# A shared row of four buffers, copies in dead tiles, and a planner with a corrected forward pass and other durations

## The chip, the cores and the metric

The kernel runs on one core of one Trainium2 chip. The metric is the device time of one execution in microseconds (us), the median of the runs; a profile is taken of one further execution. The engines are TensorE (PE, with its weight loads as PEld), VectorE (DVE), ScalarE (ACT), GpSimd (POOL) and SyncE (SP). DMA transfers are issued from three queues here: SP's, ACT's and POOL's.

## The reference

One pre-norm residual layer with two mixers on the same normalised input, in float32, for 1024 tokens of width 1024:

```python
h = rmsnorm(x, norm_w);  proj = h @ w_in
y_a = (dilated_mixture(q_a, k_a, v_a) * silu(dsa_z)) @ w_up_a      # three windows / dilations, 8 heads of 64
q, k, v = split(silu(causal_conv4(gdn_qkv)));  q, k = l2norm(q) / 8, l2norm(k)
# gated delta rule in chunks of 64, per head (8 heads of 64)
G = cumsum(g);  decay = exp(G_i - G_j) for i >= j
a = (k*beta @ k.T) * decay (strictly lower);  t_inv = inverse(I + a)
u = t_inv @ (v*beta);  w = t_inv @ (k*beta*exp(G));  attn = (q @ k.T) * decay
scan over chunks: v_new = u - w @ S;  o = (q*exp(G)) @ S + attn @ v_new
                  S = S * exp(G_last) + (k*exp(G_last - G)).T @ v_new
y_b = (rmsnorm(o) * silu(gdn_z)) @ w_up_b
out = rmsnorm(x + (sigmoid(gate_a)*y_a + sigmoid(gate_b)*y_b) @ w_out, final_norm_w)
```

## The kernel before

The projections run as units of 128-row weight blocks. A float32 weight is loaded into `wstage`, split into two float16 parts (`whi` on ACT, `wlo` on DVE), and multiplied by the split input in three products (lines 184, 185, 186). A `Feed` object streams these units, and every other stage of the kernel calls `feed.tick(n)` between its own products, so that PE always has unit work between them. Matmuls that stand at lines 184 to 186 are therefore work that fills PE while another stage waits for its operands.

Mixer A (attention) is done first, then mixer B (the delta rule), whose 8 heads are handled in two halves, `hb` 0 and 1. For each half: `decay` builds `gm` from the decays on DVE and sums it on PE (line 1195); `keys_side` and `pairs` build the matrix `a` (in `MT`) and spill it; `solve` inverts the 32 x 32 diagonal blocks on DVE in 31 steps (`stmp`, `X`, working on `As`), scales `X`, makes its negated transpose `T1`, spills both (`u_d`, `t_d`) and reloads them, shaped for PE, as blocks of `MT` (line 1335) and as `T1p` (line 1333). `merge` makes the 64 x 64 inverse from the blocks: `left` multiplies by T1p (line 1350) and DVE writes `Y`; `right` (line 1365) multiplies by Y. `state_parts` multiplies the inverse with the values (`u`, line 1413, PSUM banks G) and with the keys `kbt` (`w`, line 1417, banks S), each in two groups of four tiles. Each group has two u banks, copied out by DVE and spilled on POOL's queue, and two w banks, copied out by ACT and spilled on ACT's queue (lines 1424 to 1429). `values` transposes v and scales it into `rv`, which is spilled. A second call of `pairs` makes q times k in the same PSUM banks (line 1266, `E` on DVE afterwards). Gate units between them write `gst` on ACT and spill it on ACT's queue (`gspb`, lines 948 and 950). In the conv units, `xc` and `ca` (lines 1005 to 1021) are copied by ACT and worked on by DVE.

Buffers come from pools by tag; tiles of one tag share `bufs` buffers in turn, and a tile waits until the one that had the buffer before is read for the last time. The tag `rv` is a row of three buffers of 2 KB a partition; `Y`, `uw` and `rv` share it. `gm` has a tag of its own with two. `As`, `X` and `T1p` have one buffer each; in the second half, the first group's `kbt` lies in As and the second's in X.

PE's instructions stand in the order in which the program is written. The order of DVE, ACT, POOL and SP is made at the end of the file by a planner: `steps_of` gives each instruction a modelled duration (`Step.cost`) and its dependences, buffers included; `fill` places them in time, forward with ranks and then backward for new ranks; `orders_of` does that three times (`PASSES`) and keeps the order whose modelled end is earliest; `set_orders` fixes it. The forward `fill` takes events (time, engine) from a heap. Before, an engine with nothing ready goes either into the heap for the time of its next known instruction, or into the set `blocked`; `known`, which is called when an instruction's last dependence is placed, wakes only engines in `blocked`.

Of the kernel before, what the change touches and what calls it, by code (L numbers as in the profile page):

```python
# [11 lines left out]
F32 = mybir.dt.float32  # L12
# [66 lines left out]
def hybrid_block(ctx: ExitStack, tc: tile.TileContext, A):  # L79
# [1099 lines left out]
    def decay(hb):  # L1179

        for t in range(8):
            if hb == 0 and t < 2:

                if t == 0:
                    room = wst.tile([128, 512], F32, name="x7", tag="x7", bufs=1)
                gm = room[:, 256 * t:256 * t + 256]
            else:
                gm = p2_.tile([128, 256], F32, name="gm", tag="gm", bufs=2)
            gm = gm.bitcast(F16).rearrange("p (l a i) -> p l a i", l=2, i=64)
            TT(gm, bc(gsplit[:, :, t, hb], 64), upto64[:, None, None, :].to_broadcast([128, 2, 4, 64]), ALU.mult)  # L1190
            if t == 0:
                feed.tick(GM_LAG)
            p = bank("G", 2)
            for l in range(2):
                PE.matmul(p[:, :256], lhsT=later16, rhs=gm[:, l].rearrange("p a i -> p (a i)"), start=(l == 0),
                          stop=False)
            PE.matmul(p[:, :256], lhsT=ident_b, rhs=hide_b[:, None, :].to_broadcast([128, 4, 64]),
                      start=False, stop=True)
            SC.activation(E[hb][:, t].rearrange("p a b c -> p (a b c)"), p[:, :256], AF.Exp)
            feed.tick(2)  # L1200
# [138 lines left out]
    def merge(hb, T1p, bsp):  # L1339
# [4 lines left out]
        def left(g):  # L1344
            py = bank("S", 2)
            Y = p2_.tile([128, 16, 32], F32, name="Y", tag="rv", bufs=3)
            for n in range(16):
                for c2 in range(2):
                    r = 64 * c2
# [34 lines left out]
    def state_parts(hb):  # L1384
# [13 lines left out]
        for g in range(2):  # L1398
# [6 lines left out]
            for n in range(8):  # L1405
                t, q, o = n // 2, n % 2, n * 64
                for x in range(2):
                    for r, e in ((0, 0), (1, 1), (0, 1), (1, 0)):
# [6 lines left out]
                        else:  # L1415
                            b = 64 * e
                            PE.matmul(pw[r][b:b + 64, o:o + 64], lhsT=kb[rs, t, 2 * q + e], rhs=Ub, start=(n == 0),
                                      stop=True, skip_group_check=True)
            for x, ps2 in enumerate((pu, pw)):
                for r in range(2):  # L1420
                    c2 = r ^ hb
                    uw = p2_.tile([128, 4, 2, 64], F32, name="uw", tag="rv", bufs=3)
                    with tc.high_priority():
# [9 lines left out]
    def values(hb):  # L1433
        def then(c, vT):
            h0 = 4 * hb + 2 * c

            def turn(t0):
                p = bank("O", 1)
                for tt in range(4):
                    PE.transpose(p[:, tt * 128:tt * 128 + 128],  # L1440
                                 vT[:, 2 * (t0 + tt):2 * (t0 + tt) + 2].rearrange("p c i -> p (c i)"), ident)
                rv = p2_.tile([128, 4, 2, 64], F32, name="rv", tag="rv", bufs=3)
                with tc.high_priority():
# [505 lines left out]
TABLE_NS = 1283  # L1949
TILE_SWITCH_NS = 300  # L1950
QUEUE_NS = 4
# [47 lines left out]
class Step:  # L1999
# [17 lines left out]
    def cost(self):  # L2017
        w, r = [[x for x in self.args if x.write == y] for y in (True, False)]
        n = max(x.cols for x in self.args)
        if self.kind == "InstMatmult":  # L2020
            self.small = tuple(self.ins.tile_size) != (128, 128)
# [22 lines left out]
        elif self.eng == "DVE":  # L2044
            one = len(r) == 1
            self.ns = {"InstMemset": 60 + 0.5 * n, "InstReciprocal": 150 + 6.2 * n, "InstTensorCopy": 160 + 0.55 * n}.get(
                self.kind, 150 + 1.0417 * n)
            if self.kind == "InstTensorScalarPtr":
                self.ns = 150 + 0.53 * n if one else self.ns + 60 * (len(r) > 2)
            self.hold = self.ns - 83  # L2050
        elif self.eng == "ACT":
            self.ns = 130 + 0.9 * n
            if self.kind == "InstActivation":
                self.table = TABLES.get(str(self.ins.func).split(".")[-1], 0)
                self.ns += 25 * (w[0].size == 2) + 30 * (len(r) > 1)
            self.hold = self.ns - 90 + 40 * (len(w) > 1)
            self.ns += 100 * (len(w) > 1)
        else:
            self.hold = self.ns = 100 + 0.85 * n
# [95 lines left out]
def fill(steps, rank, back, given):  # L2155
# [4 lines left out]
    free, moved, due, open_ = [{e: x() for e in order} for x in (float, float, list, list)]  # L2160
    events, blocked, table, small, end = [(0.0, e) for e in order], set(), 0, None, 0.0

    def known(i):
# [3 lines left out]
        elif e not in given:  # L2167
            heapq.heappush(due[e], (ready[i], i))
        if e in blocked:
            blocked.discard(e)  # L2170
            heapq.heappush(events, (max(free[e], ready[i]), e))

# [13 lines left out]
    while events:  # L2186
        t, e = heapq.heappop(events)
        if t < free[e]:
            heapq.heappush(events, (free[e], e))
            continue  # L2190
        if e in given:
# [3 lines left out]
            if left[i]:  # L2195
                blocked.add(e)
                continue
            if ready[i] > t:
                heapq.heappush(events, (ready[i], e))
                continue  # L2200
        else:
# [3 lines left out]
            if not open_[e]:  # L2205
                if due[e]:
                    heapq.heappush(events, (due[e][0][0], e))
                else:
                    blocked.add(e)
                continue  # L2210
# [12 lines left out]
        order[e].append(i)  # L2223
        heapq.heappush(events, (free[e], e))
        passed(s, t, late)
# [132 lines left out]
```

## Time and profile before

| | us |
|---|---|
| runs | 1075.26, 1066.41, 1068.09 |
| median | 1068.09 |
| profiled execution, its own time | 1070.89 |
| its span, first to last instruction | 1069.1 |
| PE's sequence of the second half's merge begins at about | 721.5 |
| PE's products w of the second half end at | 750.4 |

The profile gives for each engine its busy time, for each group of instructions the time one takes and what the engine waited for before it, and for each stretch of time the clock that was granted to PE (1.00 is full). A wait is named by the instruction that waits and by what released it.

### The profile page before, as it was taken

To read this page: it belongs to the slowest core of one execution; us is meant where nothing else is said; L and a number is where in the kernel's file an instruction comes from. 1 tells how busy PE (TensorE), PEld (TensorE's weight loads), DVE (VectorE), ACT (ScalarE), POOL (GpSimd) and SP (SyncE) were. 2 spreads that over 40 slices of the span, in tenths; PEclk is the share of its full clock that TensorE was granted. 3 is DMA by queue.
4 is the path that set the end of the run, shared out by engine and by line. 5 is a ranking of instruction groups with operands and counts; after the bars stand their busy time and mean duration, and the time that the engine had idled before them with its cause. 6 is when DMAs were issued, how large, how long until landed. Compare 5 with 4: busy or idle time off the path is not lost.

```text
span 1069.1 us, 24944 instructions
## 1 busy us (share of the span) xinstructions
PE 1042.0 (97%) x9986; PEld 639.1 (60%) x9986; DVE 877.7 (82%) x2030; ACT 573.0 (54%) x1306; POOL 56.3 (5%) x107
## 2 busy tenths in 40 slices
PE   7999999999999999999999999998899999999997
PEld 5995695765957755866655545544545555444444
DVE  6898987989979889989957986885298768899934
ACT  6446767777766666567635533244244336434523
POOL 0000000000000000000000000110100000000000
PEclk9999999999999999999999999998899999999999
DMA  7144532532624432552336166784685414823132
GB/s 278 62 123 114 140 105 90 134 100 83 188 88 127 123 105 75 145 154 69 95 108 186 59 176 178 262 228 154 209 271 168 147 53 147 324 93 124 58 132 79
DMA packets 99780, 148.53 MB, mean 139 GB/s; under 512 B 31168, under 2 KB 64704, under 8 KB 98512
## 3 DMA queue, kind: packets, MB, share of 16 engines
q1 hardware_dynamic: 69264, 84.64, 27.3%
q0 software_dynamic: 12320, 44.11, 13.1%
q10 hardware_dynamic: 18080, 18.20, 5.0%
q8 instruction: 78, 1.28, 0.5%
q14 instruction: 38, 0.31, 0.1%
HBM read 91.13 MB, written 36.90 MB: 120 GB/s over the span
## 4 chain that ended last, share of the span: by engine, by line
PE 67%; DVE 14%; DMA 7%; issue 5%; ACT 4%; SPq 2%; ACTq 0%; DVEq 0%; POOLq 0%
PE ps_mm L184 16%; PE ps_mm L185 16%; PE ps_mm L186 16%; DMA wstage<-in_w 2%; PE ps_S L185 2%; PE ps_S L184 2%; PE ps_S L186 2%; DVE tl L87 1%; SPq L629 1%; DVE ca L84 1%; PE ps_G L813 1%; ACT sm L803 1%; DVE sm L799 1%; DVE wlo L84 1%; PE ps_G L184 1%
## 5 line engine op out<-in xcount | busy, mean ns | idle before, releaser
L186 PE MATMUL ps_mm<-h_hi,wlo 128*128 128x512 f16 (+1 forms) x552 | 208.8, 378 | 0.0
L184 PE MATMUL ps_mm<-h_hi,whi 128*128 128x512 f16 (+1 forms) x492 | 186.5, 379 | 0.0
L185 PE MATMUL ps_mm<-h_lo,whi 128*128 128x512 f16 (+1 forms) x492 | 186.3, 379 | 0.0
L186 PEld LDWEIGHTS <-wlo 128*128 128x128 f16 x788 | 77.4, 98 | 87.1 <-issue 1.7
L184 PEld LDWEIGHTS <-whi 128*128 128x128 f16 x848 | 83.4, 98 | 69.4 <-issue 1.7
L185 PEld LDWEIGHTS <-whi 128*128 128x128 f16 x848 | 83.3, 98 | 69.6 <-issue 3.4
L803 ACT ACTIVATE sm<-sm,osb 128x128 f32<-128x128 f32 (+1 forms) x160 | 69.3, 434 | 47.0 <-DVE osb L799 46.2
L799 DVE CUSTOM_DVE_ANT_0 sm<-ps_S,amask 128x128 f32<-128x128 f32 (+1 forms) x192 | 59.7, 347 | 6.7 <-PE ps_S L792 6.6
L87 DVE TENSOR_TENSOR tl<-ps_G,th 128x256 f16<-128x256 f32 (+1 forms) x96 | 52.0, 542 | 15.4 <-ACT th L818 14.8
L330 ACT ACTIVATE whi<-wstage 128x512 f16<-128x512 f32 x76 | 46.1, 626 | 31.3 <-DVE wstage L329 9.5
L84 DVE SCALAR_TENSOR_TENSOR wlo<-wstage,whi 128x1024 f16<-128x1024 f32 x42 | 51.0, 1220 | 8.8 <-ACT whi L167 7.3
L167 ACT ACTIVATE whi<-wstage 128x1024 f16<-128x1024 f32 x41 | 42.7, 1054 | 27.7 <-PE ps_mm L185 23.7
L185 PE MATMUL ps_mm<-wlo,h_hi 128*128 128x256 f16 (+1 forms) x256 | 57.3, 246 | 0.0
L84 DVE SCALAR_TENSOR_TENSOR ca<-xc,cw,ca 128x512 f32<-128x512 f32 x72 | 53.8, 747 | 2.5 <-ACT ca L1010 2.2
L84 DVE SCALAR_TENSOR_TENSOR whi<-wstage,whi 128x512 f16<-128x512 f32 x76 | 51.9, 687 | 3.8 <-ACT whi L330 3.4
L329 DVE TENSOR_TENSOR wstage<-wstage 128x512 f32<-128x512 f32 x76 | 52.0, 687 | 0.9
L813 PE MATMUL ps_G<-cons,sm 128*128 128x128 f32 x280 | 47.0, 274 | 2.1 <-ACT sm L803 2.0
L818 ACT CAST th<-ps_G 128x256 f16<-128x256 f32 (+1 forms) x96 | 44.1, 459 | 6.7 <-PE ps_G L813 6.2
L184 PE MATMUL ps_mm<-whi,h_hi 128*128 128x256 f16 (+1 forms) x192 | 46.5, 256 | 0.0
L186 PE MATMUL ps_mm<-whi,h_lo 128*128 128x256 f16 (+1 forms) x192 | 46.2, 255 | 0.0
L184 PE MATMUL ps_mm<-h_hi,wlo 128*128 128x512 f16 x120 | 45.6, 380 | 0.0
L185 PE MATMUL ps_mm<-h_lo,wlo 128*128 128x512 f16 x120 | 45.5, 379 | 0.0
(489 smaller groups left out, 2880.3 us busy)
## 6 DMA issues: line engine op xcount, KB each, us to landing
wstage<-in_w POOLq DMA_DIRECT2D x68, 512.0 KB, 4.5
og<-osb ACTq DMA_DIRECT2D x32, 132.0 KB, 2.4
og<-og SPq DMA_DIRECT2D x32, 132.0 KB, 2.2
gspb<-gst ACTq DMA_DIRECT2D x16, 256.0 KB, 4.3
sga<-gspa SPq DMA_DIRECT2D x8, 512.0 KB, 8.8
wstage<-in_w_up POOLq DMA_DIRECT2D x8, 512.0 KB, 4.7
sgb<-gspb SPq DMA_DIRECT2D x8, 512.0 KB, 4.0
wos<-in_w_out SPq DMA_DIRECT2D x8, 512.0 KB, 4.7
```

What stands on the lines that cost most here:

```text
L84: (eng or V).scalar_tensor_tensor(out, in0, scalar, in1, op0=op0, op1=op1)
L87: (eng or V).tensor_tensor(out, in0, in1, op)
L167: SC.activation(hi[:, 4 * c:4 * c + 4], st, AF.Copy, scale=W_SCALE)
L184: PE.matmul(out, lhsT=wh(k), rhs=mh(k), start=first and i == 0, stop=False, skip_group_check=True)
L185: PE.matmul(out, lhsT=wh(k), rhs=ml(k), start=False, stop=False, skip_group_check=True)
L186: PE.matmul(out, lhsT=wl(k), rhs=mh(k), start=False, stop=last and i == len(ks) - 1, skip_group_check=True)
L329: V.tensor_tensor(self.part[name], self.part[x], self.part[y], ALU.add)
L330: SC.activation(t[:, b, 0], self.part[name], AF.Copy, scale=W_SCALE)
L799: V.tensor_tensor_reduce(P[:, u, :128 * nk], psc[:, u * 256:u * 256 + 128 * nk], mask, -cexp, -NEG, ALU.add, ALU.min, accum_out=osb[:, 256 ...
L803: SC.activation(P[:, u, :128 * nk], P[:, u, :128 * nk], AF.Exp, bias=osb[:, 256 + hd:257 + hd], scale=-1.0, accum_out=osb[:, 260 + hd:261 ...
L813: PE.transpose(pt[:, c:c + 128], P[:, u, i * 128:i * 128 + 128], ident)
L818: SC.copy(th[:, :n], pt[:, :n])
```

## The change

It has four parts.

1. `gm` no longer has two buffers of its own but shares the row `rv`, which now has four buffers in place of three, for gm, Y, uw and rv together.
2. In the second half the w copies of a group go into one tile `ws`, which holds both, in place of two buffers of the row: the first group's in `T1p`, the second's in `As`. The spill then reads from `ws`.
3. The planner's durations: a switch of PE between tile shapes 250 ns (was 300); DVE's copies from PSUM by the slower slope; an additional term (`apart`) for DVE and ACT instructions that read a PSUM tile in single elements with a stride; ACT's instructions with a second output 190 ns more (was 100).
4. The forward pass of `fill`: each engine has a next wake-up time, and an engine that waits for a later time is woken earlier when another of its instructions becomes ready sooner.

The computation is the same.

```diff
@@ decay
-                gm = p2_.tile([128, 256], F32, name="gm", tag="gm", bufs=2)
+                gm = p2_.tile([128, 256], F32, name="gm", tag="rv", bufs=4)
@@ merge, left
-            Y = p2_.tile([128, 16, 32], F32, name="Y", tag="rv", bufs=3)
+            Y = p2_.tile([128, 16, 32], F32, name="Y", tag="rv", bufs=4)
@@ state_parts
+            if hb:
+                ws = p2_.tile([128, 2, 4, 2, 64], F32, name="ws", tag="As" if g else "T1p", bufs=1)
             for x, ps2 in enumerate((pu, pw)):
                 for r in range(2):
                     c2 = r ^ hb
-                    uw = p2_.tile([128, 4, 2, 64], F32, name="uw", tag="rv", bufs=3)
+                    if x and hb:
+                        uw = ws[:, r]
+                    else:
+                        uw = p2_.tile([128, 4, 2, 64], F32, name="uw", tag="rv", bufs=4)
                     with tc.high_priority():
                         (SC.copy if x else V.tensor_copy)(uw, ps2[r].rearrange("p (t q i) -> p t q i", q=2, i=64))
@@ values
-                rv = p2_.tile([128, 4, 2, 64], F32, name="rv", tag="rv", bufs=3)
+                rv = p2_.tile([128, 4, 2, 64], F32, name="rv", tag="rv", bufs=4)
@@ the planner
-TILE_SWITCH_NS = 300
+TILE_SWITCH_NS = 250
@@ Step.cost
+        apart = any(x.psum and x.piece == x.size for x in r) and n >= 256
...
             one = len(r) == 1
-            self.ns = {"InstMemset": 60 + 0.5 * n, "InstReciprocal": 150 + 6.2 * n, "InstTensorCopy": 160 + 0.55 * n}.get(
+            fast = one and not r[0].psum
+            self.ns = {"InstMemset": 60 + 0.5 * n, "InstReciprocal": 150 + 6.2 * n, "InstTensorCopy": 160 + (0.55 if fast else 1.0417) * n}.get(
...
+            self.ns += 0.58 * n * apart
...
-            self.hold = self.ns - 90 + 40 * (len(w) > 1)
-            self.ns += 100 * (len(w) > 1)
+            self.ns += 0.94 * n * apart + 190 * (len(w) > 1)
+            self.hold = self.ns - 90
@@ fill
-    events, blocked, table, small, end = [(0.0, e) for e in order], set(), 0, None, 0.0
+    events, wake, table, small, end = [], {}, 0, None, 0.0
+
+    def at(t, e):
+        if t < wake.get(e, np.inf):
+            wake[e] = t
+            heapq.heappush(events, (t, e))
@@ fill, known
-        if e in blocked:
-            blocked.discard(e)
-            heapq.heappush(events, (max(free[e], ready[i]), e))
+        if e is not None:
+            at(max(free[e], ready[i]), e)
@@ fill, the loop
         t, e = heapq.heappop(events)
+        if t != wake[e]:
+            continue
+        wake[e] = np.inf
         if t < free[e]:
-            heapq.heappush(events, (free[e], e))
+            at(free[e], e)
             continue
...
             if not open_[e]:
                 if due[e]:
-                    heapq.heappush(events, (due[e][0][0], e))
-                else:
-                    blocked.add(e)
+                    at(due[e][0][0], e)
                 continue
```

PE's order is the same in both kernels. The order of the others moves in three places that matter here. Of line numbers, those above 1418 are 5 higher after the change and those of the planner more.

ACT, where the second half's w copies (`uw`, then `ws`) stand with their spills `wn_d` and the gate unit's `gst` and `gspb`. Before:

```order
L1424 COPY uw<-ps_S 128x512
L1426 DMA wn_d<-uw 128x4x128
L1424 COPY uw<-ps_S 128x512
L1426 DMA wn_d<-uw 128x4x128
L1424 COPY uw<-ps_S 128x512
L948 ACTIVATE gst<-ps_mm 128x512
L1426 DMA wn_d<-uw 128x4x128
L950 DMA gspb_11041<-gst 128x512
L1424 COPY uw<-ps_S 128x512
L1426 DMA wn_d<-uw 128x4x128
```

The same place of ACT after the change:

```order
L1429 COPY ws<-ps_S 128x512 x2
L1431 DMA wn_d<-ws 128x4x128 x2
L1429 COPY ws<-ps_S 128x512 x2
L1431 DMA wn_d<-ws 128x4x128 x2
L948 ACTIVATE gst<-ps_mm 128x512
L950 DMA gspb_11039<-gst 128x512
```

The two copies of a group now stand together ahead of their two transfers, and the gate unit's copy and spill stand behind all of them.

DVE at the end of the second half's solve, from the last two steps (`stmp`, `X`) to `T` (T1 in the code); `ca` and `xc` belong to a conv unit, `wlo` to a weight unit. Before:

```order
L87 TENSOR_TENSOR stmp<-As,X 128x31
L84 SCALAR_TENSOR_TENSOR wlo<-wstage,whi 128x1024
L87 TENSOR_TENSOR X<-X,stmp 128x31
L84 SCALAR_TENSOR_TENSOR ca<-xc,cw,ca 128x512
L87 TENSOR_TENSOR X<-X,bsc 128x1024
L84 SCALAR_TENSOR_TENSOR ca<-xc,cw,ca 128x512
L1323 TENSOR_SCALAR T_9508<-X 128x1024
L84 SCALAR_TENSOR_TENSOR ca<-xc,cw,ca 128x512
L84 SCALAR_TENSOR_TENSOR wlo<-wstage,whi 128x1024
```

The same place of DVE after the change:

```order
L87 TENSOR_TENSOR stmp<-As,X 128x31
L1007 COPY xc<-xc 128x3
L87 TENSOR_TENSOR X<-X,stmp 128x31
L87 TENSOR_TENSOR X<-X,bsc 128x1024
L84 SCALAR_TENSOR_TENSOR ca<-xc,cw,ca 128x512
L1323 TENSOR_SCALAR T_9508<-X 128x1024
L84 SCALAR_TENSOR_TENSOR ca<-xc,cw,ca 128x512 x2
L1005 MEMSET xc 128x3
L84 SCALAR_TENSOR_TENSOR wlo<-wstage,whi 128x1024
```

The wlo and the ca that stood between the solve's last steps now stand behind T; with two ca from some steps earlier, four ca, one wlo and a memset that were ahead of T are behind it.

SP's queue at the second half's reloads (`MT` blocks from `u_d`, `T1p` from `t_d`, then the keys `kbt` and gate reloads `sga`). Before:

```order
L1326 DMA u_d_9510<-X 128x1024
L1327 DMA t_d_9511<-T_9508 128x1024
L1335 DMA MT_8544<-u_d_9510 32x32x32 x4
L1333 DMA T1p<-t_d_9511 32x32x32 x2
L1393 DMA kbt<-kb_d_8558 128x1024 x2
```

The same place of SP's queue after the change:

```order
L1326 DMA u_d_9510<-X 128x1024
L1327 DMA t_d_9511<-T_9508 128x1024
L1335 DMA MT_8544<-u_d_9510 32x32x32
L1333 DMA T1p<-t_d_9511 32x32x32 x2
L1335 DMA MT_8544<-u_d_9510 32x32x32 x2
L1393 DMA kbt<-kb_d_8558 128x1024
L1335 DMA MT_8544<-u_d_9510 32x32x32
L1393 DMA kbt<-kb_d_8558 128x1024
```

Both T1p loads now stand behind one MT load in place of four, and the last MT load stands between the two kbt loads.

More of the change, by code (lines that the diff above doesn't have):

```diff
@@ L2195, in fill @@
             if left[i]:
-                blocked.add(e)
                 continue
             if ready[i] > t:
-                heapq.heappush(events, (ready[i], e))
+                at(ready[i], e)
                 continue
@@ L2206, in fill @@
                 if due[e]:
-                    heapq.heappush(events, (due[e][0][0], e))
-                else:
-                    blocked.add(e)
+                    at(due[e][0][0], e)
                 continue
@@ L2223, in fill @@
         order[e].append(i)
-        heapq.heappush(events, (free[e], e))
+        at(free[e], e)
         passed(s, t, late)
```

## The prediction

> **What bounds the kernel now.** I read the page's head first, then the waits of TensorE (PE), then a table of stretches around the two longest waits, then the chain and the queues inside them.
>
> ```profile
> span 1069.1 us, 24944 instructions
> PE 1042.0 (97%) x9986; PEld 639.1 (60%) x9986; DVE 877.7 (82%) x2030; ACT 573.0 (54%) x1306; POOL 56.3 (5%) x107
> PEclk9999999999999999999999999998899999999999
> ...
> PE ps_mm L502 <- DVE nwd L87: 5.2, 1, 5.2
> PE ps_S L1350 <- DMA T1p<-t_d: 3.6, 2, 2.9
> PE ps_S L1266 <- ACT uw L1424: 3.5, 1, 3.5
> PE ps_G L813 <- ACT sm L803: 2.0, 2, 1.4
> PE ps_mm L184 <- ACT gst L948: 1.5, 1, 1.5
> PE ps_O L840 <- DVE tl L87: 1.3, 2, 0.9
> ```
>
> PE is the bound: 1042.0 of 1069.1 us, so at most 27 us can be had by waiting less. The clock row has two digits below 9, side by side, in slices 28 and 29 of 40, 722 to 775 us. The wait rows give total, times and longest: after the 5.2 us of the start, the two largest are a load of T1p that PE's merge waits for, and a copy of ScalarE (ACT) that frees a PSUM bank. The stretches around them (columns: length, busy time of PE, its weight loads, DVE, ACT and POOL with counts, granted clock, DMA share, GB/s):
>
> ```profile
> 650.00:706.00 56.00, 56.00 (x754) 29.09 (x755) 48.55 (x103) 18.45 (x31) 7.78 (x13) 1.00 0.65 213
> 706.00:721.50 15.50, 15.50 (x195) 8.30 (x186) 12.69 (x22) 4.81 (x10) 1.65 (x3) 1.00 1.06 293
> 721.50:724.80 3.30, 0.55 (x3) 0.05 (x1) 1.99 (x4) 2.65 (x6) 0.00 (x0) 1.00 0.99 217
> 724.80:731.60 6.80, 5.95 (x73) 3.26 (x74) 4.91 (x8) 1.48 (x4) 0.00 (x0) 0.50 0.68 266
> 731.60:753.00 21.40, 21.40 (x520) 12.87 (x519) 8.29 (x13) 7.96 (x15) 4.26 (x7) 1.00 0.35 107
> 753.00:755.50 2.50, 0.32 (x3) 0.19 (x2) 0.00 (x0) 0.00 (x0) 0.80 (x2) 1.00 0.91 219
> 755.50:762.30 6.80, 5.45 (x71) 3.14 (x72) 1.29 (x2) 0.59 (x1) 0.56 (x1) 0.50 0.42 144
> ...
> 374.20:534.50 160.30, 157.23 (x1538) 104.09 (x1536) 150.38 (x480) 106.86 (x281) 7.42 (x14) 1.00 0.38 107
> ```
>
> Each wait is followed by 6.8 us at clock 0.50. So a wait costs its own length and a dip. Two ways to size it. By windows: 721.5 to 731.6 is 10.1 us, in which PE did 0.55 us of work at full clock and 5.95/2 at half, so 6.6 us were lost; 753.0 to 762.3 is 9.3 us with 0.32 + 5.45/2 of work, so 6.3 lost; 12.9 in all. By waits: 3.6 + 3.5, and half of 6.8 twice, 13.9. I take 13.5, an estimate between them.
>
> The waits of 1.5 us and less have no dip after them, the shortest one with a dip has 2.9. The Trainium skill, page "TensorE: Matmul & The Clock Gate", Part 1, section on the clock gate, says that the array falls to half rate after at least one whole idle window of about 3.4 us and comes back after a busy one of that length. Here two idle windows would have to lie in waits of 2.9 and 3.5 us, and the trace decides otherwise for the first.
>
> **First part of the change: row of four, copies elsewhere.** No instruction is added or taken away, and the order of PE is the same; what can change is when PE's operands are there. For the second stall, the chain and ACT's rows:
>
> ```profile
> 750.26 0.12 PE ps_S L1417 x8
> ...
> 756.21 0.59 ACT uw L1424
> 756.85 1.98 PE ps_S L1266 x62
> ...
> 744.41 0.59 ACT L1424 COPY uw<-ps_S 128x512 f32<-128x512 f32 x1 [1.44 <-PE ps_S L1417]
> 747.50 0.59 ACT L1424 COPY uw<-ps_S 128x512 f32<-128x512 f32 x1 [2.50 <-DMA wn_d<-uw]
> 751.10 0.59 ACT L1424 COPY uw<-ps_S 128x512 f32<-128x512 f32 x1 [3.02 <-DMA wn_d<-uw]
> 756.21 0.59 ACT L1424 COPY uw<-ps_S 128x512 f32<-128x512 f32 x1 [3.80 <-DMA gspb<-gst]
> ```
>
> The products end at 750.38. Three of the four copies waited for a DMA: the row of three had no free buffer until an earlier spill had read it. That the last row names the gate spill gspb only says which DMA ended last; the two copies before it, held by wn_d, show the kind. With ws the copies of a group have a tile each. As and T1p are dead there: the kbt in As is read by the first group's products, T1p by the merge. In the new order two copies stand in a row, then two DMAs. So both banks are free at 750.38 + 2 x 0.59 = 751.6, and PE wants them at 753.0: 1.4 us to spare. The gst that stood between them comes 0.6 us later at most; its bank is not wanted sooner than ACT's next gst, so I cost it at nothing. The cover is those 1.4 us; if it goes, the stall is the shortfall. What is late next is E (DVE waits for the same L1266 products), which only comes earlier.
>
> ACT had the same wait one half earlier, and DVE paid for it:
>
> ```profile
> 684.11 0.59 ACT L1424 COPY uw<-ps_S 128x512 f32<-128x512 f32 x1 [9.56 <-DMA wn_d<-uw]
> ...
> 685.22 0.17 DVE L1007 COPY xc<-xc 128x3 f32<-128x3 f32 x1 [3.45 <-ACT xc L1008]
> ```
>
> The copies of xc queue behind that copy on ACT, and DVE sat 3.45 us in the middle of the triangular solve. A fourth buffer lets it go by up to 3.45 us; the low end is 0, if the fourth is just as late (gm, Y, rv and u now share the row). I take 3.45, since for this group only four w and four u copies compete in it.
>
> **Second part: the planner moves DVE and SP.** The solve's end and T1p's way:
>
> ```profile
> 702.89 1.22 DVE L84 SCALAR_TENSOR_TENSOR wlo<-wstage,whi 128x1024 f16<-128x1024 f32 x1
> 704.14 0.74 DVE L84 SCALAR_TENSOR_TENSOR ca<-xc,cw,ca 128x512 f32<-128x512 f32 x1
> 705.93 0.75 DVE L84 SCALAR_TENSOR_TENSOR ca<-xc,cw,ca 128x512 f32<-128x512 f32 x1
> 706.60 1.05 DVE L1323 TENSOR_SCALAR T<-X 128x1024 f32<-128x1024 f32 x1
> ...
> 706.08 5.49 DMA u_d<-X
> ...
> 719.54 6.37 DMA T1p<-t_d
> 725.96 1.91 PE ps_S L1350 x62
> ...
> 711.59 5.15 SPq L1335 DMA_DIRECT2D MT<-u_d  x4
> 716.79 3.88 SPq L1333 DMA_DIRECT2D T1p<-t_d  x2
> ...
> t_d<-T SPq DMA_DIRECT2D x1, 512.0 KB, 5.1
> ```
>
> By the order, five instructions and a small memset that stood ahead of T (T1 in the code) now stand behind it: one wlo of 1.22 and four ca of about 0.75 (the wlo and two of the ca are in the rows), 4.2 us. So T, which ended at 707.65, ends at 703.4, and with the 3.45 from above at 700.0. (Two further wlo of 1.22 move into DVE's idle time ahead of the solve; they are left as margin.) Then T1p's way: the spill of T, 5.1 to landing; the T1p issues on SP, 3.88 at most; their landing, 6.37. SP has one MT load ahead of them in place of four, which took 5.15, and that one waits for u_d, spilled before T, so it adds nothing. From T's end that is 15.4 us: T1p is there at 715.4, or at 718.8 without the 3.45. PE wants it at about 722 (0.55 us of work after 721.5): 6.6 or 3.2 us to spare. What covers the load is PE's other work, full in the row 706.00:721.50. The MT loads now behind T1p, and a kbt load that goes between them, wait for two T1p issues and a kbt issue more, at most 3.88 and 1.3 (taken as a quarter of the 5.15), against 4.2 to 7.7 gained; I cost it at nothing. The next to be late would be those MT loads, for the right products. POOL's row of transfers keeps its order but for one or two places, and no term rests on it.
>
> **Third part: everything else that the new costs move.** The decays' gm now take rv buffers.
>
> ```profile
> 588.27 0.69 DVE L87 TENSOR_TENSOR gm<-wide,cons 128x512 f16<-128x512 f16 x1 [0.93 <-PE ps_G L1195]
> ...
> 599.17 0.68 DVE L87 TENSOR_TENSOR rv<-ps_O,bg 128x512 f32<-128x512 f32 x1
> ```
>
> The last gm comes 11 us before the first rv, and what holds it is PE's own product with the gm before, so with four buffers for two it can only come sooner: by the 0.93 of DVE's idle time at most, and PE does not wait for it. The other end is one lap of a buffer held by a spill, ACT's 9.56 above. I take nothing, as no rv, Y or u is alive then. In the attention stretch 374 to 534, and in the one before it, 39 of the 96 tl stand later in the new order and 18 earlier, mostly by one instruction. The waits for sm, gst and tl are 4.8 us in all (2.0 + 1.5 + 1.3, rows above). Bounds: 4.8 gained if all went, as much lost if each doubled. I take 0, the middle.
>
> **Sum.** 13.5 gone, 0 elsewhere. Against its own time, 1070.89 for the profiled execution (span 1069.1 and 1.8 around it), that is 1057.4. The median of the runs is 1068.09, 2.8 below the profiled one. If that difference is a dip less (half of 6.8 is 3.4), the saving is already partly in it and 1057.4 stands; if it is spread over everything, 1068.09 - 13.5 = 1054.6. I take the middle, 1056.0.
>
> **The rivals.** (a) Only one stall goes. For the first: DMA share is 1.06 in 706 to 721.5, so T1p may land late for want of engines, whatever its place in the queue; it decides once the landing takes 3.2 to 6.6 us longer. For the second: 1.4 us to spare is little. Against: the u_d and MT traffic comes earlier too, into 690 to 706, and the row 650.00:706.00 has a share of 0.65. It gives 1056.0 plus 6.3 to 6.6: 1062.5.
>
> (b) The stalls go, the dips stay, because the small 32x32 products and not the waiting bring the clock down. Against: the other half's merge and products lie in 650 to 706, and that row has clock 1.00. It gives 1056.0 + 2 x 3.4 = 1062.8. By the rule of the Trainium skill's page named above, a wait shorter than a whole window would not lower the clock, so the first dip would have such another cause and one dip would stay; that case is in this rival, at 1059.4.
>
> (c) The change doesn't do what it says: the waits move but stay, because the row of four fills as the row of three did and the costs are no nearer the chip's. Time as before, 1068. Against: the ws tiles wait for nothing in the order.
>
> (d) Slower: DVE becomes the bound in the attention stretch. It is busy 150.38 of 160.30, PE 157.23. DVE has 9.9 us of idle time there to make good what is late; if each of the 39 later tl in the two stretches held PE by 0.65, the mean of the two tl waits of before, 25 us would be added and it would be 1056.0 + 25 = 1081. It decides from 23 us of new waits on (1078.8 - 1056.0). Against: PE waited for tl twice in 96 before.
>
> **How the numbers follow.** Chances: my forecast 0.62, (a) 0.17, (b) 0.08, (c) 0.06, (d) 0.07. Faster or slower by over 1% (10.7 us, about what a measurement of this kernel can tell from no change) means up to 1057.4 or from 1078.8. The forecast's own spread is 1051 (all 4.8 of small waits go too) to 1060 (some are added); about 0.54 of its 0.62 lie below 1057.4, and a little of (b). Faster 0.55, within 1% 0.38, slower 0.07. The range has the forecast and rivals (a) and (b) within 1051 to 1064 and leaves out (c), (d) and a few hundredths.
>
> **What would show it.** Right: no PE wait on T1p or on the w copies above 1 us, clock 1.00 from 650 to 780, the T1p load landing before 720, the four w copies in pairs with no idle time for a DMA before the second of each, and DVE's 3.45 at 685 gone. Wrong: a new wait of over 2.4 us anywhere, with its dip; tl waits growing in 374 to 534; or T1p landing more than 8 us after its issue.

## The result and the profile after

| | before | after |
|---|---|---|
| runs, us | 1066.41, 1068.09, 1072.51, 1075.26 | 1055.29, 1055.89, 1056.34, 1057.15 |
| median | 1070.30 | 1056.12 |
| profiled execution: span | 1069.1 | 1055.4 |

The ratio after to before is 0.9866, with a 95% interval of 0.9819 to 0.9912: 1.3% faster. The predicted time was 1056.0.

The head of the page of the changed kernel, and PE's waits (total, times, longest):

```profile
span 1055.4 us, 24937 instructions
PE 1036.0 (98%) x9986; PEld 636.2 (60%) x9986; DVE 876.9 (83%) x2030; ACT 577.0 (55%) x1306; POOL 56.1 (5%) x107
PEclk9999999999999999999999999999999999999999
...
PE ps_mm L502 <- DVE nwd L87: 5.3, 1, 5.3
PE ps_G L813 <- ACT sm L803: 2.4, 2, 1.7
PE ps_mm L184 <- ACT gst L948: 2.0, 1, 2.0
PE ps_mm L478 <- DVE h_lo L84: 1.0, 1, 1.0
```

Both long waits are gone from PE's list, and both digits below 9 from the clock row. What is left at the top is the start, two waits for `sm` (the attention's scores on ACT), and one wait for `gst` that has grown from 1.5 to 2.0 us. The same stretches as before:

```profile
706.00:721.50 15.50, 15.50 (x180) 8.21 (x171) 8.64 (x14) 6.53 (x15) 1.07 (x2) 1.00 1.00 305
721.50:724.80 3.30, 3.30 (x75) 1.99 (x74) 3.17 (x6) 1.76 (x4) 0.00 (x0) 1.00 0.17 71
724.80:731.60 6.80, 6.80 (x178) 3.95 (x178) 6.67 (x11) 3.39 (x7) 0.00 (x0) 1.00 0.28 109
731.60:753.00 21.40, 21.40 (x503) 12.99 (x497) 6.29 (x10) 5.70 (x11) 5.81 (x10) 1.00 0.60 159
753.00:755.50 2.50, 2.50 (x15) 1.42 (x14) 1.98 (x3) 2.07 (x5) 0.88 (x2) 1.00 0.94 303
755.50:762.30 6.80, 6.80 (x39) 3.88 (x38) 2.43 (x4) 3.40 (x7) 0.69 (x2) 1.00 0.86 318
```

PE is full in each of them at clock 1.00. The DMA share is still 1.00 ahead of 721.5, as it was (1.06), but T1p is no longer among the transfers that PE waits for.

PE executes the same 9986 matmuls in the same order in both kernels, so the start of the n-th can be compared one by one. Where the difference changes:

| place (time before) | after minus before there, us | step | what it is |
|---|---|---|---|
| up to 361 | -3.1 | -3.1 | waits for a load of keys (Ks, 225), for tl (290 and 361), and 0.4 at the start, gone |
| 388 to 393 | -0.95 | +2.1 | the wait for gst 0.45 longer, and a dip of the clock behind it, 1.7 |
| 474 | -0.56 | +0.4 | the wait for sm longer |
| 722 to 731 | -6.57 | -6.0 | the wait for T1p and its dip |
| 753 to 762 | -13.10 | -6.5 | the wait for the w copies and its dip |
| end | about -13.7 | -0.6 | small ones |

So the two places of the prediction gave 12.5 us, and everything else 1.2.

How T1p came early: DVE's solve, SP's queue and PE's first product with T1p, and the transfers' median landing times, of the changed kernel:

```profile
654.20 0.19 DVE L87 TENSOR_TENSOR stmp<-As,X 128x31 f32<-128x31 f32 x1
693.02 1.23 DVE L87 TENSOR_TENSOR X<-X,bsc 128x1024 f32<-128x1024 f32 x1
694.82 1.05 DVE L1323 TENSOR_SCALAR T<-X 128x1024 f32<-128x1024 f32 x1
...
700.09 0.32 SPq L1335 DMA_DIRECT2D MT<-u_d  x1
701.61 2.76 SPq L1333 DMA_DIRECT2D T1p<-t_d  x2
704.42 4.93 SPq L1335 DMA_DIRECT2D MT<-u_d  x2
...
t_d<-T SPq DMA_DIRECT2D x1, 512.0 KB, 5.7
T1p<-t_d SPq DMA_DIRECT2D x2, 128.0 KB, 8.1
...
721.74 1.20 PE L1350 MATMUL ps_S<-T1p,MT 32*32 32x32 f32 x64
```

T ends at 695.87, 11.8 us earlier than before (707.65), and its loads are out at 704.4, so that T1p has landed at 710.7 (issued at 702.0, 8.7 us on the way), 11.0 us ahead of PE. And the w copies of ACT in the second half:

```profile
737.62 1.08 ACT L1429 COPY ws<-ps_S 128x512 f32<-128x512 f32 x2 [1.44 <-PE ps_S L1417]
743.64 1.07 ACT L1429 COPY ws<-ps_S 128x512 f32<-128x512 f32 x2 [4.94 <-PE ps_S L1417]
```

Each pair waits for PE's products alone, and not for a transfer. The second is done at 744.7; PE wants its banks at 746.28 (the first product of `pairs` in the chain). That is 1.6 us to spare, where 1.4 had been worked out.

### The profile page after: what moved, and what is told of

Its sections match the earlier page's. It is cut to its first block, busy times and chain, and to the rows that moved or that the text cites. A ratio compares the mean times of both kernels' runs of the same rounds, so it can differ in the third digit from the quotient of the medians.

```text
span 1055.4 us, 24937 instructions
## 1 busy us (share of the span) xinstructions
PE 1036.0 (98%) x9986; PEld 636.2 (60%) x9986; DVE 876.9 (83%) x2030; ACT 577.0 (55%) x1306; POOL 56.1 (5%) x107
## 3 DMA queue, kind: packets, MB, share of 16 engines
q8 instruction: 78, 1.28, 0.5%
## 4 chain that ended last, share of the span: by engine, by line
PE 90%; DVE 4%; ACT 2%; DMA 2%; issue 1%; SPq 0%; ACTq 0%; DVEq 0%
PE ps_mm L184 22%; PE ps_mm L185 22%; PE ps_mm L186 22%; PE ps_G L813 3%; PE ps_S L186 2%; PE ps_S L184 2%; PE ps_S L185 2%; PE ps_S L792 1%; PE ps_S L790 1%; PE ps_G L185 1%; PE ps_G L186 1%; PE ps_G L184 1%; PE ps_S L1711 1%; PE ps_G L1739 1%; DMA Ks<-pcl 1%
## 5 line engine op out<-in xcount | busy, mean ns | idle before, releaser
L813 PEld LDWEIGHTS ps_G<-cons,sm 128*128 128x128 f32 x280 | 35.4, 142 | 17.1 <-ACT sm L803 3.6
```

The lines of the kernel that those rows point to most:

```text
L813: PE.transpose(pt[:, c:c + 128], P[:, u, i * 128:i * 128 + 128], ident)
```

## The experiments

All were compared with runs of the kernel before on the same chip. The kernel before spreads from 1063 to 1077 us there, so the ratios are what counts; a part of the reason for that spread is at the end.

**The two halves of the change, apart.** First the buffers alone, with the old planner (the part of the diff from `decay` to `values`):

> The four buffers and ws with the planner of before (old durations, old forward pass). SP still has all four MT loads ahead of T1p, and the work on DVE ahead of T is 0.7 us more than in the changed kernel. Theory A (either half of the change is enough for the first stall, the buffers alone take the second): T ends about 1 us later than in the changed kernel (696.9 against 695.9), T1p lands at about 715, ahead of the 721.8 at which PE wants it; no wait on T1p, none on the w copies, clock 1.00 from 650 to 780, and 1055 to 1058 us, within 2 us of the changed kernel's 1056.1. Theory B (the planner's new durations and pass are what takes the first stall away, by the order of SP and the work ahead of T): a wait on T1p of over 2 us with its dip stays, and the time is about 1062 to 1063.

Measured: 1058.28 (1057.68 to 1061.85), ratio 0.9877 [0.9848, 0.9906]. PE has no wait on T1p and none on the w copies. SP's order was the old one (four MT loads ahead of T1p), as these rows of its queue, and of PE, show:

```profile
703.39 2.23 SPq L1335 DMA_DIRECT2D MT<-u_d  x4
705.72 2.51 SPq L1333 DMA_DIRECT2D T1p<-t_d  x2
...
725.90 1.20 PE L1350 MATMUL ps_S<-T1p,MT 32*32 32x32 f32 x64
```

T ended at 701.3, and the four MT issues took 2.2 us there. T1p would even at its 10.3 us to landing have been in place before 725.9. Theory A holds, with a median 0.3 above its range; T was later than expected (701.3 against 696.9, PE itself being 4 us later), which left the wait gone all the same. Then the planner alone, with the old buffers (`TILE_SWITCH_NS`, `Step.cost` and `fill`):

> The new durations and forward pass with the buffers of before (row of three, gm in its own two, no ws). By the order T1p stands behind one MT load and DVE has the changed kernel's work ahead of T, but ACT's w copies still alternate with their spills. Theory A: the first stall goes (T1p lands by about 719 at the latest), the second stays in some form, a PE wait of 2.5 to 3.5 us on the w copies and a dip of the clock: about 1062 to 1063. Theory B (the planner does all): both go, about 1056. Theory C (neither part does it alone): both stay, about 1069.

Measured: 1062.31 (1059.64 to 1065.29), ratio 0.9899 [0.9868, 0.9931]. From its waits of PE:

```profile
PE ps_S L1266 <- ACT uw L1424: 2.8, 2, 2.4
PE ps_mm L184 <- ACT gst L948: 2.0, 1, 2.0
```

No wait on T1p, and the second wait stays with 2.4 us at the longest and a dip. Theory A again: either half takes the first stall away, and only the buffers take the second.

**The buffers, apart.** The changed kernel without ws:

```diff
-            if hb:
-                ws = p2_.tile([128, 2, 4, 2, 64], F32, name="ws", tag="As" if g else "T1p", bufs=1)
...
-                    if x and hb:
-                        uw = ws[:, r]
-                    else:
-                        uw = p2_.tile([128, 4, 2, 64], F32, name="uw", tag="rv", bufs=4)
+                    uw = p2_.tile([128, 4, 2, 64], F32, name="uw", tag="rv", bufs=4)
```

> The changed kernel without ws: the second half's w copies take buffers of the row of four. Theory A1 (a row of four is enough; its two copies of a group stand together in the order, and the first group's spills have about 6 us until the second group): no wait of PE over 1 us on the w copies, 1056 to 1057. Theory A2 (ws is what takes the second stall away): ACT's copies of the second group wait 2 to 4 us for a spill, PE waits 2 us or more for the last of them, with a dip: about 1061 to 1063.

Measured: 1056.86 (1056.60 to 1057.61), ratio 0.9858 [0.9834, 0.9882], the same as the whole change. ACT's last two w copies:

```profile
742.59 0.59 ACT L1424 COPY uw<-ps_S 128x512 f32<-128x512 f32 x1 [4.94 <-PE ps_S L1417]
744.78 0.59 ACT L1424 COPY uw<-ps_S 128x512 f32<-128x512 f32 x1 [1.61 <-DMA un_d<-uw]
```

The very last does wait 1.6 us for a spill of u, and ends at 745.4; PE hardly feels it (under 0.2 us), as its 1.6 us to spare are just used up. So with the row of four and the new planner, ws is not what makes the gain; it is margin. Then the changed kernel with the row of three (`bufs=4` back to 3, gm back to its own tag with two), and ws kept:

> The changed kernel with ws, but with a row of three and gm in two buffers of its own, as before. Theory A1 (the fourth buffer only shortens ACT's and DVE's wait in the first half, and the work taken from ahead of T is enough for T1p): ACT waits some 9 us in the first half again, T ends about 3.5 us later than in the changed kernel, T1p lands at about 715, no PE wait; 1056 to 1057. Theory A2 (the fourth buffer is needed for the first stall): T1p lands after 722, PE waits 2 us or more for it, with a dip: about 1061 to 1063.

Measured: 1057.05 (1056.52 to 1060.05), ratio 0.9864 [0.9837, 0.9892], again the same. ACT waits 5.0 us in the first half (not 9), T ends at 698.8, 3 us later than in the changed kernel, and PE does not wait for T1p. And ws alone in the kernel before, with row, planner and durations as they were:

> The kernel before with ws alone: row of three, gm in its own two, old durations, old pass. By the order T has the same 35 us of other DVE work ahead of it as before, and four MT loads stand ahead of T1p. Theory A (ws takes the second stall and nothing else; the first goes only with the fourth buffer or the planner): no PE wait on the w copies of the second half, the wait on T1p of about 3.5 us with a dip stays: 6 to 7 us below the kernel before, 1063 to 1065. Theory B (the first stall hangs on the second half's copies too, through the row): both go, 1057 to 1059.

Measured: 1064.16 (1060.08 to 1070.50), ratio 0.9939 [0.9913, 0.9966]. From its waits of PE:

```profile
PE ps_S L1350 <- DMA T1p<-t_d: 2.5, 1, 2.5
PE ps_G L813 <- ACT sm L803: 1.9, 2, 1.3
PE ps_S L1417 <- ACT uw L1429: 1.6, 1, 1.6
```

The second stall is gone, the first stays. Theory A. The last row is not the second stall: it is a wait at 686.6, in the first half, where ACT's copy waits 11.06 us for a spill in place of 9.56. 0.61% of 1070.57 is 6.5 us (3.6 to 9.3 by the interval); that fits the 6.5 of the second stall with its dip in the table above, though the new wait of 1.6 us is in it too.

**The first stall's terms, one at a time, in the kernel before.** On SP's queue, by hand after the planner, the two T1p loads behind the first MT load:

```diff
+    q = orders["SP"]
+    late = [i for i in q if at(i, True, "T1p_") and at(i, False, "t_d1")]
+    first = next(i for i in q if at(i, True, "MT1_") and at(i, False, "u_d1"))
...
+    orders["SP"] = q[:n] + late + q[n:]
```

> The kernel before with one thing moved: on SP's queue the two T1p loads stand behind one MT load in place of four. Theory A (the queue's order alone is a large enough term: 4 to 5 us of the load's way): T1p's issues begin when T's spill has landed, at about 712.8, the last is out at about 715.5 and lands at 722; PE waits 0 to 1 us for it with no dip behind, the second stall stays as it was (about 3.5 us and a dip): 6 to 7 us below the kernel before of the same chip, ratio 0.994. Theory B (the transfers are held back by full DMA engines, whatever their place): T1p still lands at 724 to 726, PE waits 2 us or more, the time is that of before within 2 us.

Measured: 1066.03 (1062.71 to 1069.74), ratio 0.9974 [0.9951, 0.9996]. T1p was out at 716.0 and PE did not wait for it, as theory A said. But only 2.8 us (0.4 to 5.2 by the interval) were gained of the 6 to 7. The waits of PE from 680 to 760, and the stretch after the merge:

```profile
PE ps_S L1266 <- ACT uw L1424: 2.2, 2, 1.9
PE ps_G L1365 <- DVE Y L87: 1.6, 3, 0.7
...
735.00:739.50 4.50, 4.50 (x52) 2.58 (x45) 0.77 (x2) 1.15 (x2) 0.00 (x0) 0.65 0.10 38
```

Now PE waits for Y, the next step of the same chain. DVE has the same four instructions ahead of Y in both kernels (a sum of squares rq, a whi, a wstage, a ca), but comes to them later here: rq starts at 724.22, 1.4 us behind PE's first product with T1p (722.81), and Y at 726.93. In the changed kernel rq starts at 720.58, 1.2 us ahead of that product (721.74), and Y at 723.29, right behind the products. Moving the loads does not hasten DVE: its T ends at 708.48 here, against 695.87, and rq waits for a copy of ACT that stands behind conv work of DVE. The rows of rq and Y, first here, then in the changed kernel:

```profile
724.22 0.69 DVE L1251 TENSOR_REDUCE rq<-ps_O 128x8 f32<-128x512 f32 x1 [1.27 <-ACT ps_O L1250]
726.93 1.41 DVE L87 TENSOR_TENSOR Y<-ps_S,pack 32x512 f32<-32x512 f32 x2
```

```profile
720.58 0.69 DVE L1251 TENSOR_REDUCE rq<-ps_O 128x8 f32<-128x512 f32 x1 [2.11 <-ACT ps_O L1250]
723.29 1.41 DVE L87 TENSOR_TENSOR Y<-ps_S,pack 32x512 f32<-32x512 f32 x2
```

And a dip (0.65 over 4.5 us) came all the same, behind waits of 0.4 to 0.7 us. Next, DVE's work behind T (four ca, one wlo and a memset), SP's queue left alone:

```diff
@@ DVE, order of the kernel before
-L84 SCALAR_TENSOR_TENSOR wlo<-wstage,whi 128x1024
 L87 TENSOR_TENSOR X<-X,stmp 128x31
-L84 SCALAR_TENSOR_TENSOR ca<-xc,cw,ca 128x512
 L87 TENSOR_TENSOR X<-X,bsc 128x1024
-L84 SCALAR_TENSOR_TENSOR ca<-xc,cw,ca 128x512
 L1323 TENSOR_SCALAR T_9508<-X 128x1024
...
+L84 SCALAR_TENSOR_TENSOR wlo<-wstage,whi 128x1024
+L84 SCALAR_TENSOR_TENSOR ca<-xc,cw,ca 128x512 x3
```

> The kernel before with one thing moved: four ca, one wlo and a memset of DVE stand behind T in place of ahead of it; SP's queue as before, four MT loads ahead of T1p. Theory A (DVE's work ahead of T is worth its 4.2 us): X ends some 3.5 us and T some 4.2 us earlier, T1p lands about 3.5 to 4 us earlier, at 722; PE waits 0 to 1 us, no dip, the second stall stays: 6 to 7 us below the kernel before of the same chip, ratio 0.994. Theory B (the freed time is lost again to full DMA engines or to waits of the four MT issues): T1p at 724 or later, a wait of 2 us or more, the time of before within 2 us.

Measured: 1069.23 (1065.47 to 1073.11), ratio 0.9999 [0.9974, 1.0023]: no gain. The waits of PE from 680 to 760:

```profile
PE ps_S L1266 <- ACT uw L1424: 3.2, 1, 3.2
PE ps_G L1365 <- DVE Y L87: 1.6, 3, 0.7
PE ps_S L1266 <- ACT qT L1021: 1.4, 1, 1.4
PE ps_G L1266 <- ACT qT L1021: 1.1, 1, 1.1
PE ps_S L1417 <- ACT uw L1424: 1.0, 1, 1.0
PE ps_O L1247 <- DVE rq L1251: 0.4, 1, 0.4
```

The wait on T1p is gone here too. In its place PE waits 2.5 us for qT, which is made from the ca that were moved, and 1.6 for Y. Neither theory had that: the ca ahead of T were not free to wait. Nor did T come 4.2 us earlier: it ended at 706.47, 1.2 us earlier than before, since DVE's idle time in mid-solve grew from 3.45 to 5.62 us. T1p landed 7.2 us earlier (718.7 against 725.9) mostly because its transfers and their issues were faster: u_d took 2.6 us in place of 5.5, the four MT issues 2.44 in place of 5.15. In the changed kernel PE has no wait at all from 680 to 760, with the same five instructions behind T. There the solve starts earlier (654.2 against 660.2 here). The fourth buffer is not needed for that: with the row of three the solve starts at 652.9, and PE has no such wait either. That the earlier start is what makes the room is argued; no run has it alone.

**The planner's two parts.** Old durations with the new forward pass, and new durations with the old pass, both with the new buffers:

> The changed kernel's buffers and corrected forward pass with the old durations. Both stalls are gone by the buffers. Theory A (what the planner gives besides the two stalls is small, about 2 us between the buffers alone, 1058.3, and the whole change, 1056.1, and comes from the corrected pass): 1055.5 to 1057. Theory B (it comes from the durations): 1057.5 to 1059, with waits for tl near 290 and 361 as in the kernel before.

> The changed kernel's buffers and new durations with the old forward pass; DVE has 34.3 us of other work ahead of T (30.7 in the changed kernel) and four MT loads stand ahead of T1p. Theory A (the fourth buffer alone takes the first stall): T ends at about 699.5, T1p lands at about 719, ahead of 722, no wait: 1056 to 1059. Theory B (34.3 us of work and the old order of the queue together are too much even with four buffers): PE waits 1 us or more for T1p: 1060 to 1063. Of the planner's parts: the wait for gst near 387 was 1.5 with the old pass and old durations, 3.1 with the new pass and old durations, 2.0 with both new; 1.5 to 2 here would say that the new pass moved it and the durations took part of that back.

| durations | forward pass | median, us | ratio to the kernel before | largest new wait of PE |
|---|---|---|---|---|
| old | old | 1058.28 (1057.68 to 1061.85) | 0.9877 [0.9848, 0.9906] | none over 2 |
| old | new | 1060.56 (1057.51 to 1064.80) | 0.9924 [0.9890, 0.9959] | gst, 3.1 |
| new | old | 1062.33 (1059.26 to 1064.56) | 0.9928 [0.9903, 0.9954] | Ks, 4.4 in four waits |
| new | new | 1056.12 and 1057.89 | 0.9866 [0.9819, 0.9912] and 0.9883 [0.9851, 0.9915] | gst, 2.0 |

The wait rows behind the second and third line:

```profile
PE ps_mm L184 <- ACT gst L948: 3.1, 1, 3.1
```

```profile
PE ps_S L790 <- DMA Ks<-pcl: 4.4, 4, 2.8
...
PE ps_mm L184 <- ACT gst L948: 1.2, 1, 1.2
```

Neither part shows a gain by itself; each alone puts a longer wait somewhere in the attention stages. Together their medians are 0.4 to 2.2 us below the old pair, but the ratios do not tell them apart, so on top of the buffers the times show no gain of the planner. That the pass alone is the source (theory A of the first) is refuted. Theory B has the direction, since with the new pass the new durations are worth 2.7 to 4.4 us by the medians, though the intervals overlap here too; its waits for tl did not come back. What the profile has in their place is 1.1 us more of waiting for gst, which is too little for the whole difference. The wait for gst belongs to the pass: 1.5 and 1.2 us with the old one, 3.1 and 2.0 with the new. In the second kernel there is no wait on T1p, so the buffers are enough for it even with 34.3 us of work ahead of T: T1p lands at 725.0, 2.8 us ahead of PE, which is itself 6 us late there. Its 1062.33 lies in the range of theory B, but not by B's mechanism: the time goes to the waits for Ks near 295, which neither theory had.

**The wait that the change made longer.** In the changed kernel PE waits 2.0 us for gst at 385. By hand, ACT's copy of the PSUM bank and gst go ahead of two sm:

```diff
@@ ACT, order of the changed kernel
-L803 ACTIVATE sm,osb<-sm,osb 128x256
-L367 COPY ps_mm<-ps_mm 128x512
-L803 ACTIVATE sm,osb<-sm,osb 128x256
-L948 ACTIVATE gst<-ps_mm 128x512
+L367 COPY ps_mm<-ps_mm 128x512
+L948 ACTIVATE gst<-ps_mm 128x512
+L803 ACTIVATE sm,osb<-sm,osb 128x256 x2
```

> The changed kernel with two instructions of ACT moved: at about 385 us the copy of a PSUM bank and the gate unit's gst stand ahead of two sm in place of behind and between them. Theory A (PE's wait of 2.0 us there is ACT's order, and it may draw a dip of 3.4 us at half clock behind it): the wait falls to about 1.1 us, no dip near 390 in any profile, 0.9 us gained in every run and 1.7 more in those that had the dip: 1053.5 to 1055.5. Theory B (the sm that come later hold PE at L813 instead): a new wait of 0.5 to 1 us at L813 near 388, and no gain: 1056 to 1057.

Measured: 1055.11 (1054.63 to 1058.55), ratio 0.9878 [0.9850, 0.9906]. The wait is 1.2 us, no new wait for sm appears, and the clock stays at 1.00 there. Repeated beside the changed kernel, on one chip:

> The changed kernel unaltered, on the same chip and in the same rounds as the next one: 1055 to 1057.5; runs with a clock of 0.999 at 1055 to 1056, each dip behind the wait for gst of 2.0 us near 387 adding 1.7 us.

> The changed kernel with the two instructions of ACT moved (the PSUM copy and gst ahead of two sm). Theory A: 0.8 us below the changed kernel in runs without a dip and 1 to 2 us below it in the median, 1054.5 to 1055.5. Theory B (no gain): the same as the changed kernel within 0.5 us.

Measured: 1057.89 (1055.95 to 1060.31) for the changed kernel, and 1056.36 (1055.16 to 1057.28) for the one with gst first; ratios to the kernel before 0.9883 [0.9851, 0.9915] and 0.9865 [0.9834, 0.9897]. Both medians lie above their expected ranges. Side by side the lowest runs differ by 0.8 and the medians by 1.5; the first time the medians differed by 1.0, on different chips. The intervals overlap, so a gain of about 1 us is likely from the waits (2.0 against 1.2) and not proved by the times. Its 1055.11 is the lowest median of this study, but its ratios (0.9878 and 0.9865) are no better than that of the changed kernel without ws (0.9858).

## Why the prediction was right

Point by point, by its own steps:

- *The two stalls with their dips, 13.5 us, estimated between 12.9 and 13.9.* They measured 12.5 (6.0 and 6.5), so the windows (6.6 and 6.3) came nearer than the sum of the waits and half of each dip: part of each wait lies within its dip (0.9 us of the first, 1.3 of the second), and is counted twice in that sum.
- *The second stall: banks free 1.4 us before PE wants them.* 1.6 measured. That ws is what moves it was too narrow: with the new planner the row of four does the same without it (1056.86), and ws alone does it too.
- *The first stall: T1p at 715.4 for a T that ends at 700.0.* The way from T's end was right in its sum, 15.4 us forecast and 14.8 measured, but two of its three terms were off and cancelled, which was luck: the spill took 5.7 us (5.1 in the forecast), the issues held the last load up by 0.4 (3.88), and it landed in 8.7 (6.37). That last number is past one of the forecast's own signs of being wrong, over 8 us from issue to landing. T's end was 4.1 us too late in the forecast. The solve's earlier start had no term: it began at 654.20 in place of 660.43, 6.2 us earlier, as its first steps now stand ahead of a Y that waits for PE. Of the 7.65 us that were to be saved before T's end, 5.55 came; a Y and an rv (2.1 us) now lie within the solve. That made the margin 11.0 us in place of 6.6, so nothing hung on it. The forecast also took DVE's 4.2 us as free; by the experiment that moved them alone they are not.
- *ACT's 3.45 us in the first half.* The wait of 9.56 is gone with four buffers, and 5.5 are left of it with the planner alone. Right in kind.
- *Everything else 0, within 4.8 either way.* 1.2 us gained in the profiles: waits of 3.1 went, and 2.5 came at 388 and 474. The shift at 388 is the one place where a wait grew into a dip; the forecast had no dip among these terms, and whether one comes depends on where the wait falls (last section). That the sum came out at 13.7 between the two profiled executions (1070.89 and 1057.15), where 13.5 was forecast, is also two errors that cancel: 1.0 too much for the stalls, 1.2 too little for the rest.
- *Rivals.* Late T1p through full DMA engines fell: the share was again 1.00 in that stretch, and the landing took 2.3 us longer than forecast, where 3.2 to 6.6 would have decided. The rival that the small products bring the dips fell for both dips of the kernel before: the 3.41 us ahead of each held no 32x32 product, and 2.73 and 2.18 us of PE's idle time. It is not nothing, though. In the changed kernel the same products ran at 1.00, but in the two kernels with a term moved by hand a dip came behind waits of only 0.4 to 0.7 us among them (last section). DVE as the bound of the attention stretch fell: PE's waits from 374 to 535 are for gst and sm, none for tl.
- *The step from the profiled time to the median.* It was put halfway, for want of knowing whether the 2.8 us between them was a dip. The runs point to dips for most of it (last section). So the middle, and with it the agreement of 1056.0 and 1056.12, was luck as much as reasoning: 1057.4 from the profiled one and 1056.1 measured lie 1.3 apart, and the median of the kernel before has itself moved from 1068.09 to 1070.30 with a fourth run.

## What to carry to other kernels

Price a stall with what follows it: here waits of 3.6 and 3.5 us cost 6.0 and 6.5, since the clock fell behind each. Where a stall has several causes in a row (a buffer, an order, a queue), ask of each whether it alone suffices; here the fourth buffer (beside ws), or the planner, took the first stall away, and the fourth buffer (beside the planner) or two dead tiles the second, so ws, the fourth buffer or the planner could each be left out with both stalls still gone. The row of four alone, in the kernel before, was not run. And an instruction moved by hand helps little while its engine as a whole is late: the next step of the chain, and those who need what was moved, wait in its place.

## What the runs showed of the hardware

The spread of the kernel before goes mostly with the clock. It was run 54 times beside the experiments: the two runs with a mean granted clock of 0.998 took 1063.1 and 1064.2 us, twenty with 0.992 took 1069.4 to 1075.1, 1072.4 on average, two with 0.991 took 1075.0 and 1076.9, and those between lie between on average. These are 8.8 us apart, of which the lower clock by itself accounts for some 6.4 (0.006 of 1069), an estimate. In other kernels it is not all: with T1p's loads moved by hand, the longest of ten runs, 1069.7, had 0.998. The best of the kernel before, 1063.1 with hardly a dip, less the two waits of 7.1, is 1056.0, near the changed kernel's 1056.1 (its lowest is 1055.3).

Whether a wait draws a dip is not settled by its length. The stretch of 3.4 us behind the wait of 2.00 us for gst, in the changed kernel and in the one without ws, and behind the wait of 3.06 us with the old durations:

```profile
388.00:391.40 3.40, 3.40 (x13) 1.77 (x12) 2.06 (x8) 0.59 (x2) 0.00 (x0) 0.54 0.24 82
```

```profile
388.00:391.40 3.40, 3.40 (x29) 1.99 (x28) 2.46 (x9) 1.09 (x3) 0.00 (x0) 1.00 0.31 112
```

```profile
391.00:394.40 3.40, 3.40 (x29) 1.99 (x28) 1.72 (x5) 0.94 (x2) 0.00 (x0) 1.00 0.24 80
```

The same wait of 2.00 us was followed by clock 0.54 in one and by 1.00 in the other, and 3.06 us by 1.00. Each dip lasted 3.41 us, or twice that in the profile before. One can therefore count off stretches of 3.41 us from the start of a dip, forward and back through the execution, and add up PE's idle time in each (its length less PE's busy time):

| profile | stretch, us | PE idle in it, us | clock in the next stretch |
|---|---|---|---|
| before, the wait on T1p | 721.37 to 724.78 | 2.73 | 0.50 |
| changed kernel, all of the wait for gst | 384.89 to 388.30 | 2.00 | 0.50 |
| buffers alone, a wait for sm | 474.83 to 478.24 | 1.78 | 0.50 |
| planner alone, a wait for sm | 472.06 to 475.47 | 1.77 | 1.00 |
| old durations, the wait for gst cut in two | 386.12 to 389.53 and 389.53 to 392.95 | 1.77 and 1.28 | 1.00 |
| without ws, the wait for gst cut in two | 383.14 to 386.56 and 386.56 to 389.97 | 0.68 and 1.33 | 1.00 |
| T1p's loads moved by hand, 64 products 32x32 | 732.94 to 736.35 | 1.19 | 0.50 |

In all 14 profiles, from 25 to 1040 us, each of the 11 stretches with 1.78 us of idle time or more was followed by a dip. Of the others only three were, with 1.19 to 1.31 us, and each of them held 64 of the merge's 32x32 products. So here the bound is near 1.78 of 3.41 us, about half, and lower among these small products, and a wait of 3.06 us went without a dip because it was cut in two. This was read off afterwards; no run was made to test it, and PE's busy time is modelled, so the hundredths are rough.

This agrees with windows of that length that run freely, as the Trainium skill's page "TensorE: Matmul & The Clock Gate" has them in Part 1, and a wait then dips or not by where it falls. It doesn't agree with the rule in the same part of the Trainium skill's page that a whole window must be idle: waits of 2.0 and 2.9 us were enough, and 1.78 us of idle time in one stretch.
